# Attention and convolution under a written order on VectorE and ScalarE, with the sink as a column and the convolution's elementwise work off GpSimd

## The chip, the cores and the metric

The kernel runs on one core of a Trainium2 chip. The metric is the device time of one execution in microseconds. Three runs before the change gave 1163.16, 1163.87 and 1164.9 us, a median of 1163.87.

## The reference, cut to what matters

One layer of a diffusion backbone over 1024 latent tokens of width 1024, with 256 context tokens in front: a modulated RMSNorm; half of the width goes through attention in a window with a sink, the other half through a gated convolution of width 3; one output projection; then a mixture of 16 experts. The change lies in the attention, the convolution and the loads of the output projection's weights:

```python
scale = hd ** -0.5                                   # hd = 64: 0.125
s_loc = einsum('bnqkgd,bnjkd->bnkgqj', qb, kb) * scale        # |i - j| <= 128
s_ctx = einsum('bnqkgd,bjkd->bnkgqj', qb, k_ctx) * scale      # all 256 context keys
p = softmax(concatenate([sk, s_ctx, s_loc], axis=-1), axis=-1)   # sk: one sink value a head
out = einsum(..., p_ctx, v_ctx) + einsum(..., p_loc, vb)

u = cg * hv                                          # convolution
up = pad(u, ((0, 0), (1, 1), (0, 0)))
y = conv_w[0] * up[:, :-2] + conv_w[1] * up[:, 1:-1] + conv_w[2] * up[:, 2:]
return bg * y

x = x + gt1 * (concatenate([att, conv], axis=-1) @ w_out)
```

## The kernel before

All products are made of float32 operands split into a high and a low part of a faster type: the high part is a rounded copy (ScalarE), the low part the difference (VectorE or GpSimd), and three matmuls (high by high, high by low, low by high) stand for one. A tile's name with an h or an l at its end is its high or low part.

The stage of the change is the one in which attention and convolution are woven together. `attention()` (line 680) runs 33 rounds for 32 units; unit u is the query block b = u // 4 of 128 tokens and the head pair hp = u % 4. In round u the generators `scores(u)` and `values(u - 1)` are advanced alternately, six steps a round. `scores` multiplies the queries with 256 context keys and 256 or 384 latent keys into PSUM (`ps_s`, lines 563 and 565), once for each of the two heads; VectorE adds the mask and takes the row's maximum, sink included (line 575), ScalarE takes exp and its sum (line 578), a few instructions on two columns add the sink's share (lines 585 to 588), and the two heads are scaled, one on VectorE (line 594), one on ScalarE (line 592). `values` turns the probabilities on TensorE (`pt`, line 622) in two or three pieces, splits each piece (`pth`, high on ScalarE in line 625, low on VectorE in line 626), multiplies with the values (`po_att`, line 613) and joins the product's two halves: a copy on ScalarE (`up`, line 639) and two additions on VectorE (`attT`, line 643).

`conv()` (line 714) runs 12 parts: for each of four groups f of 128 channels the products for cg, hv and bg, each of two halves of 512 tokens with 8 steps of three matmuls (lines 730 to 732). `conv_load` (line 701) loads the next part's weights (`wcr`) and splits them whole: the high part on ScalarE, the low part on GpSimd (line 711). After hv the three taps are applied: line 755 and twice line 760 on GpSimd, line 759 on ScalarE. `weave` (line 815) advances attention and convolution in turn; after the last unit `prepare()` (line 798) takes attention's place: it loads the output weights in four pieces (`wo_load`: DMA, then a multiplication with the gate row in line 776, the tiles `wor`) and splits them (`wo_split`, lines 223 and 224, `woh` and `wol`). Then `project(0)` multiplies (line 879): the first 24 matmuls take pieces 0 and 1, the next 24 pieces 2 and 3.

In this stage the order on TensorE alone is that of the code (`manual_schedule(engines={ET.PE})`, line 94). On the other engines a scheduler sets it, by a timeline that it simulates while the kernel is built; at run time each engine takes its instructions in that order, and each waits for what it reads.

Of the kernel before, what the change touches and what calls it, by code (L numbers as in the profile page):

```python
# [85 lines left out]
def tile_layer(ctx, tc, x, c, cx, c_ctx, w_ada, b_ada, g_mix, w_in, conv_w, sink, w_out, g_ffn,  # L86
# [188 lines left out]
    nc.sync.dma_start(sinkb, sink.partition_broadcast(128).rearrange("p o h -> p (o h)"))  # L275
    nc.vector.tensor_scalar(sink8, sinkb, 8.0, None, op0=OP.mult)

# [262 lines left out]
    attT = {}  # L540
    negm = consts.tile([128, NT, NH], F32, name="negm")
    mx = consts.tile([128, NT, NH], F32, name="mx")
# [8 lines left out]
    def scores(u):  # L551
# [4 lines left out]
        loc = slice(blocks[0] * 128, (blocks[-1] + 1) * 128)  # L556
        sm2, s_sm = slots.get((2, 640), F32, "sm")
        for i in range(2):
# [37 lines left out]

    ptf = [0]

    def values(u):
        b, hp = divmod(u, 4)  # L600
        kv = hp // 2
# [33 lines left out]

        if b // 4 not in attT:
            attT[b // 4] = slots.get((4, 512), F32, "attT")
        up = work.tile([64, 2, 128], F32, tag="up", name="up")
        nc.scalar.copy(up.rearrange("p b c -> p (b c)"), po[64:128])
        pov = po.rearrange("p (b c) -> p b c", b=2)  # L640
        for par in range(2):
            dst = attT[b // 4][0][64 * par:64 * par + 64, hp, (b % 4) * 128:(b % 4 + 1) * 128]
            nc.vector.tensor_tensor(dst, pov[:64, par], up[:, par], op=OP.add)
        if b % 2 and hp == 3:
            slots.put(qT[b // 2][1])

# [33 lines left out]
    def attention():  # L680
        rc = router_consts()
        for u in range(4 * NT + 1):
            if u == 2:
                q_turn(NT - 1)
            if 20 <= u < 24:
                next(rc, None)
            sc = scores(u) if u < 4 * NT else iter(())
            va = values(u - 1) if u else iter(())

            for i, g in enumerate((sc, va, sc, va, va, va)):  # L690
                next(g, None)
                if i < 5:
                    yield 1
                if u == 0 and g is sc:
                    yield 1

# [4 lines left out]
    def conv_load(i):  # L701

        if i >= 12:
            return
        f, part = divmod(i, 3)
        raw = wm("wcr", (8, 128))
        c0 = conv_col[part] + f * 128
        nc.sync.dma_start(raw, win_v[:, :, c0:c0 + 128])
        wsp, s_w = slots.get((2, 8, 128), F32R, "wcs")
        nc.scalar.copy(wsp[:, 0], raw)  # L710
        nc.gpsimd.tensor_tensor(wsp[:, 1], raw, wsp[:, 0].bitcast(F32), op=OP.subtract)  # L711
        conv_w_of[i] = (wsp, s_w)

    def conv():
        st = {}
        conv_load(0)
        for i in range(12):
            f, part = divmod(i, 3)
            conv_load(i + 1)
            wsp, s_w = conv_w_of.pop(i)  # L720
            if part == 0:
# [4 lines left out]
            for half in range(2):  # L726
                ps = p1n("ps_cv")
                for k in range(KC):
# [3 lines left out]
                    mm(ps, wsp[:, 1, k], hi, start=False, stop=k == KC - 1)  # L732
                    yield 1
                tok = slice(half * 512, (half + 1) * 512)
# [5 lines left out]
                else:  # L740
                    if f == 2 and half == 0:
                        cvT[1] = slots.get((2, S), F32, "cvT")
                    dst = st["y"] if f == 0 else cvT[f // 2][0][:, f % 2]
                    nc.vector.tensor_tensor(dst[:, tok], ps, st["y"][:, tok], op=OP.mult)
            slots.put(s_w)
            if i == 2:
# [5 lines left out]
            if part == 1:  # L752
                y = st["cg"].rearrange("p a b -> p (a b)")
                u = st["u"]
# [14 lines left out]

    def wo_load(i):  # L770

        g, n = divmod(i, 2)
        cols = slice(n * 512, (n + 1) * 512)
        r, s_r = slots.get((4, 512), F32, "wor")
        nc.sync.dma_start(r, wout_v[:, 4 * g:4 * g + 4, cols])
        nc.vector.tensor_tensor(r, r, crow["gt1"][:, None, cols].to_broadcast([128, 4, 512]), op=OP.mult)
        wo[g, n] = [r, s_r]

# [19 lines left out]
    def prepare():  # L798
# [3 lines left out]
        bcast_row(crow["gt1"], rows_d[0])  # L802
        wo_load(0)
        yield 4
        wo_split(0)
        attended(0, ((0, 4),))
        wo_load(1)
        yield 8
        wo_split(1)
        attended(0, ((4, 2),))  # L810
        yield 6
        wo_load(2)
        yield 4

    weave([(steps(attention(), prepare()), 160.0), (conv(), 161.0)])

# [681 lines left out]
def _constants():  # L1498
# [10 lines left out]
    amask = np.zeros((128, 768), np.float32)  # L1509
    amask[:, 256:384] = np.where(j >= q, 0.0, NEG)  # L1510
    amask[:, 512:640] = np.where(j <= q, 0.0, NEG)
    amask = amask.astype(ml_dtypes.bfloat16)
# [33 lines left out]
```

## Time and profile before

| | |
|---|---|
| runs | 1163.16, 1163.87, 1164.9 us |
| the profiled execution | 1163.48 us, of which its instructions span 1161.7 us |
| TensorE busy in the span | 1058.4 us (91%) |
| VectorE, ScalarE, GpSimd busy | 967.2 (83%), 766.1 (66%), 351.0 us (30%) |
| attention and convolution | 178.4 to 433.7 us of the span |
| output projection, routing and sorting | 433.7 to some 560 us |
| experts | from there to the end |

A group's line gives its source line, engine, operation, what it writes and reads, its count, then its busy time, the mean duration of one, and the idle time of the engine just before it with what ended it. A timeline's line gives the start, the duration, the engine and the source line, and in brackets how long the engine had been idle and who released it. Matmuls overlap, so a matmul's duration is longer than its distance to the next.

### The profile page before, as it was taken

How to read it: one execution, taken by the hardware profiler on the slowest of the kernel's cores; microseconds unless marked ns; L12 is line 12 of the kernel's file. 1: busy time of each engine (PE TensorE's matmuls, PEld its weight loads, DVE VectorE, ACT ScalarE, POOL GpSimd, SP SyncE). 2: the span in 40 equal slices, each digit the busy share in tenths (PEclk: the TensorE clock that was granted, in tenths of full speed). 3: DMA queues.
4: the chain of work that ended last, by engine and by line, in shares of the span. 5: the costliest groups of instructions: out<-in, count | busy, mean ns of one | idle time of the engine just before them, and what ended most of it. 6: DMA issues, size and time to landing. Idle time of an engine off the chain costs nothing.

```text
span 1161.7 us, 15615 instructions
## 1 busy us (share of the span) xinstructions
PE 1058.4 (91%) x5486; PEld 873.5 (75%) x5486; DVE 967.2 (83%) x1661; ACT 766.1 (66%) x1058; POOL 351.0 (30%) x292
## 2 busy tenths in 40 slices
PE   6786889999899998999399999999999999999981
PEld 2675667888788877888288888888888888888861
DVE  7888455887878785389899999999999999999975
ACT  7565655767666643232288878878878877888853
POOL 0457681221303031222212433322333322330022
PEclk9897999999999999999599999999999999999996
DMA  9644440010101079648789999999999999999555
GB/s 376 232 164 144 164 146 19 24 33 1 55 1 37 19 278 339 181 127 270 273 322 356 399 403 390 391 388 389 395 404 392 389 389 389 394 404 390 203 195 221
DMA packets 90790, 292.89 MB, mean 252 GB/s; under 512 B 7044, under 2 KB 20816, under 8 KB 89688
## 3 DMA queue, kind: packets, MB, share of 16 engines
q1 hardware_dynamic: 84808, 270.40, 61.0%
q0 software_dynamic: 5904, 21.50, 7.7%
q8 instruction: 43, 0.70, 0.2%
q14 instruction: 35, 0.29, 0.1%
HBM read 266.69 MB, written 25.18 MB: 251 GB/s over the span
## 4 chain that ended last, share of the span: by engine, by line
PE 72%; DVE 13%; issue 5%; ACT 4%; DMA 4%; POOL 1%; POOLq 0%; ACTq 0%; DVEq 0%; SPq 0%
PE pg L1313 14%; PE pu L1313 14%; PE py L1313 13%; PE po L879 7%; PE ps_cv L731 3%; PE ps_cv L730 3%; PE ps_cv L732 3%; PE pt L622 2%; PE po_att L613 2%; DVE whl L1150 2%; PE ps_s L565 2%; PE xTp L1299 1%; PE ps_s L563 1%; PE pl L954 1%; PE hTtp L1299 1%
## 5 line engine op out<-in xcount | busy, mean ns | idle before, releaser
L1150 DVE TENSOR_TENSOR whl<-raw,whl 128x1024 fp32r<-128x1024 f32 x384 | 455.2, 1224 | 29.9 <-ACT whl L1147 18.9
L1147 ACT CAST whl<-raw 128x1024 fp32r<-128x1024 f32 x384 | 400.2, 1054 | 100.2 <-PE pu L1313 35.6
L1313 PE MATMUL pg<-whl,xT 128*128 128x512 f32 x768 | 186.2, 395 | 2.1 <-DVE whl L1150 2.1
L1313 PE MATMUL pu<-whl,xT 128*128 128x512 f32 x768 | 180.9, 392 | 0.0
L1313 PEld LDWEIGHTS pg<-whl,xT 128*128 128x128 f32 x768 | 142.3, 189 | 31.6 <-DVE whl L1150 2.9
L1313 PE MATMUL py<-whl,hTt 128*128 128x512 f32 x720 | 165.9, 389 | 0.0
L1313 PEld LDWEIGHTS pu<-whl,xT 128*128 128x128 f32 x768 | 143.0, 188 | 29.4
L1313 PEld LDWEIGHTS py<-whl,hTt 128*128 128x128 f32 x720 | 135.1, 188 | 28.4 <-DVE whl L1150 0.3
L1278 POOL TENSOR_SCALAR oh<-iota,pos 128x128 bf16<-128x128 f32 x104 | 100.5, 981 | 0.5
L1371 POOL DMA_INDIRECT acc_d<-yt,idx x15 | 38.5, 2565 | 196.0 <-DVE yt L1359 196.0
L1323 POOL DMA_INDIRECT xr<-h_d,idx x16 | 22.3, 1395 | 199.2 <-DVE gate_w L1289 199.2
L730 PE MATMUL ps_cv<-hTh,wcs 128*128 128x512 f32 x192 | 81.5, 424 | 0.0
L463 POOL TENSOR_TENSOR acc<-acc,wmod 128x1024 f32<-128x1024 f32 x28 | 70.0, 2518 | 27.8 <-ACT wmod L461 26.7
L625 ACT CAST pth<-pt 128x512 fp32r<-128x512 f32 (+1 forms) x88 | 46.1, 524 | 46.2 <-PE pt L622 46.1
L731 PE MATMUL ps_cv<-hTl,wcs 128*128 128x512 f32 x192 | 76.1, 397 | 0.0
L732 PE MATMUL ps_cv<-hTh,wcs 128*128 128x512 f32 x192 | 76.0, 396 | 0.0
L879 PE MATMUL po<-woh,ah 128*128 128x512 f32 x240 | 70.8, 404 | 0.6 <-ACT woh L223 0.6
L626 DVE TENSOR_TENSOR pth<-pt,pth 128x512 fp32r<-128x512 f32 (+1 forms) x88 | 53.9, 613 | 20.1 <-ACT pth L625 19.2
L711 POOL TENSOR_TENSOR wcs<-wcr,wcs 128x1024 fp32r<-128x1024 f32 x12 | 28.6, 2389 | 110.2 <-ACT wcs L710 87.5
L578 ACT ACTIVATE sm<-sm,negm 128x640 f32<-128x640 f32 (+1 forms) x64 | 51.6, 807 | 4.0 <-DVE negm L577 3.9
L575 DVE CUSTOM_DVE_ANT_0 sm<-ps_s,maskt,sink 128x640 f32<-128x640 f32 (+1 forms) x56 | 48.3, 863 | 6.9 <-PE ps_s L565 6.3
L879 PEld LDWEIGHTS po<-woh,ah 128*128 128x128 f32 x240 | 44.1, 191 | 9.4 <-ACT woh L223 1.0
(297 smaller groups left out, 1828.4 us busy)
## 6 DMA issues: line engine op xcount, KB each, us to landing
raw<-in_w_gate_dram SPq DMA_DIRECT2D x64, 1024.0 KB, 9.6
raw<-in_w_up_dram SPq DMA_DIRECT2D x64, 1024.0 KB, 7.8
raw<-in_w_down_dram SPq DMA_DIRECT2D x64, 1024.0 KB, 9.6
wmod<-in_w_ada_dram SPq DMA_DIRECT2D x32, 512.0 KB, 3.7
wa<-in_w_ada_dram SPq DMA_DIRECT2D x8, 1024.0 KB, 5.3
wcr<-in_w_in_dram SPq DMA_DIRECT2D x12, 512.0 KB, 3.8
xt<-in_x_dram SPq DMA_DIRECT2D x4, 1024.0 KB, 20.6
wor<-in_w_out_dram SPq DMA_DIRECT2D x4, 1024.0 KB
```

Source lines behind the costliest of these rows:

```text
L463: nc.gpsimd.tensor_tensor(acc, acc, wt, op=OP.add)
L575: nc.vector.tensor_tensor_reduce(dst, src, mk, op0=OP.add, op1=OP.max, scale=1.0, scalar=sink8[:, h:h + 1], accum_out=mx[:, b, h:h + 1])
L578: nc.scalar.activation(sm, sm, AF.Exp, bias=negm[:, b, h:h + 1], scale=0.125, accum_out=esum[:, b, h:h + 1])
L626: nc.vector.tensor_tensor(pth[:, 1, :n], pt[:, :n], pth[:, 0, :n].bitcast(F32), op=OP.subtract)
L730: mm(ps, wsp[:, 0, k], hi, start=k == 0, stop=False)
L731: mm(ps, wsp[:, 0, k], lo, start=False, stop=False)
L732: mm(ps, wsp[:, 1, k], hi, start=False, stop=k == KC - 1)
L879: mm(po[n], a, wo[k // 4, n][j][:, k % 4], start=first, stop=last)
L1147: nc.scalar.copy(w[:, 0], t[:, k % 2])
L1150: low = nc.vector.tensor_tensor(w[:, 1], t[:, k % 2], w[:, 0].bitcast(F32), op=OP.subtract)
L1278: nc.gpsimd.tensor_scalar(oh[:, t], iota1, pos[:, t, 0, e:e + 1], None, op0=OP.is_equal)
L1313: mm(ps[n], a_hl[:, a, k], w[:, j, n * 512:(n + 1) * 512], start=first, stop=last)
```

## The change

The sink becomes one more column of the scores, so the exp's own sum contains it and lines 585 to 587 go; the scale of -1/8 is multiplied into the queries, so the row's minimum serves directly as exp's bias and line 577 goes. The convolution's low parts and taps 1 and 2 move from GpSimd to VectorE, tap 0 to ScalarE, and the weights are split in halves at given steps of the part before. The order of VectorE and ScalarE in the woven stage is that of the code. In it the first head's exp stands with its scores, the second head's exp and the scaling stand one step later each, and the join of a unit's halves (`join`) is put into the next round, behind that round's first exp. `prepare()` issues the loads of the output weights apart from their gating.

```diff
@@ q_proj
-        nc.scalar.copy(qs[:, :, 0, :], tv)
-        nc.vector.tensor_tensor(qs[:, :, 1, :], tv, qs[:, :, 0, :].bitcast(F32), op=OP.subtract)
+        nc.scalar.activation(qs[:, :, 0, :], tv, AF.Copy, scale=-0.125)
+        nc.vector.scalar_tensor_tensor(qs[:, :, 1, :], tv, -0.125, qs[:, :, 0, :].bitcast(F32), op0=OP.mult,
+                                       op1=OP.subtract)
@@ scores
+        def exp(i):
+            h = 2 * hp + i
+            sx = sm2[:, i, :W + 1]
+            nc.scalar.activation(sx, sx, AF.Exp, bias=mx[:, b, h:h + 1], scale=-1.0,
+                                 accum_out=esum[:, b, h:h + 1])
...
-            nc.vector.tensor_tensor_reduce(dst, src, mk, op0=OP.add, op1=OP.max, scale=1.0,
+            if i == 0:
+                nc.vector.tensor_copy(sm2[:, :, W], sink8[:, hs])
+            nc.vector.tensor_tensor_reduce(dst, src, mk, op0=OP.add, op1=OP.min, scale=1.0,
                                            scalar=sink8[:, h:h + 1], accum_out=mx[:, b, h:h + 1])
-            nc.vector.tensor_scalar(negm[:, b, h:h + 1], mx[:, b, h:h + 1], -0.125, None, op0=OP.mult)
-            nc.scalar.activation(sm, sm, AF.Exp, bias=negm[:, b, h:h + 1], scale=0.125,
-                                 accum_out=esum[:, b, h:h + 1])
             if i == 0:
-                yield
-        hs = slice(2 * hp, 2 * hp + 2)
-        r = rec[:, b, hs]
-        nc.vector.tensor_tensor(r, sinkb[:, hs], negm[:, b, hs], op=OP.add)
-        nc.scalar.activation(r, r, AF.Exp)
-        nc.vector.tensor_tensor(r, r, esum[:, b, hs], op=OP.add)
-        nc.vector.reciprocal(r, r)
+                exp(0)
+            yield
+        exp(1)
+        yield
+        nc.vector.reciprocal(rec[:, b, hs], esum[:, b, hs])
@@ attention
-            for i, g in enumerate((sc, va, sc, va, va, va)):
-                next(g, None)
...
+            next(sc, None)
+            while joined:
+                joined.pop()()
+            yield 1
+            next(va, None)
+            yield 1
+            next(sc, None)
+            yield 1
+            next(va, None)
+            next(sc, None)
+            yield 1
...
+            next(va, None)
+            next(sc, None)
+            yield 1
+            next(va, None)
@@ conv_load, conv
+    def conv_split(i, low, n):
+        if i < 12:
+            raw, wsp, _ = conv_w_of[i]
+            ks = slice(4 * n, 4 * n + 4)
+            if low:
+                nc.vector.tensor_tensor(wsp[:, 1, ks], raw[:, ks], wsp[:, 0, ks].bitcast(F32), op=OP.subtract)
+            else:
+                nc.scalar.copy(wsp[:, 0, ks], raw[:, ks])
...
-        nc.scalar.copy(wsp[:, 0], raw)
-        nc.gpsimd.tensor_tensor(wsp[:, 1], raw, wsp[:, 0].bitcast(F32), op=OP.subtract)
...
+                    at = 8 * half + k
+                    if at in (7, 8, 9, 10):
+                        conv_split(i + 1, *divmod(at - 7, 2))
+                    if part == 2 and at in (1, 4):
+                        j = 1 if at == 1 else 2
+                        nc.vector.scalar_tensor_tensor(st["y"], st["u"][:, j:j + S], convT_w[:, 4 * j + f:4 * j + f + 1],
+                                                       st["y"], op0=OP.mult, op1=OP.add)
...
-                nc.gpsimd.tensor_scalar(y, u[:, 0:S], convT_w[:, f:f + 1], None, op0=OP.mult)
-                tap = wm("tap", (S,))
-                for j in (1, 2):
-                    w = convT_w[:, 4 * j + f:4 * j + f + 1]
-                    nc.scalar.activation(tap, u[:, j:j + S], AF.Copy, scale=w)
-                    nc.gpsimd.tensor_tensor(y, y, tap, op=OP.add)
+                nc.scalar.activation(y, st["u"][:, 0:S], AF.Copy, scale=convT_w[:, f:f + 1])
@@ prepare
-        wo_load(0)
+        wo_issue(0)
+        yield 5
+        wo_issue(1)
+        wo_gate(0)
+        attended(0, ((0, 4),))
         yield 4
         wo_split(0)
...
+        yield 5
+        wo_issue(2)
+        wo_gate(1)
+        attended(0, ((4, 2),))
+        yield 4
         wo_split(1)
...
-    weave([(steps(attention(), prepare()), 160.0), (conv(), 161.0)])
+    with tc.manual_schedule(engines={ET.PE, ET.DVE, ET.Activation}):
+        weave([(steps(attention(), prepare()), 160.0), (conv(), 161.0)])
```

Three places show how the order moves. First ScalarE in one round of the woven stage, before; `sm_2238` holds the scores of that round's unit, `pth` and `up` are of the unit before it.

```order
COPY up<-po_att 64x256
CAST pth<-pt 128x512
ACTIVATE sm_2238,esum<-sm_2238,negm 128x640
CAST pth<-pt 128x512
ACTIVATE sm_2238,esum<-sm_2238,negm 128x640
ACTIVATE rec<-rec 128x2
CAST pth<-pt 128x256
ACTIVATE sm_2238<-sm_2238,rec 128x640
```

The same of the changed kernel, in the round of unit 6 (`sm_1810`), into which one tap of the convolution falls (`cg<-u`).

```order
ACTIVATE sm_1810,esum<-sm_1810,mx 128x641
COPY up<-po_att 64x256
ACTIVATE cg<-u,smallT 128x1024
CAST pth<-pt 128x512 x2
ACTIVATE sm_1810,esum<-sm_1810,mx 128x641
CAST pth<-pt 128x256
ACTIVATE sm_1810<-sm_1810,rec 128x640
```

The copy `up` and the first `pth` stood ahead of the first exp; now the first exp stands ahead of both, and the tap between them.

Second, VectorE in a round before (`ISA` is the masked row maximum and the read of its accumulator; the round's last rows, a reciprocal and a scaling, are left out).

```order
ISA sm_2472,mx<-ps_s,maskt,sink_285 128x640
ISA mx 128x1
TENSOR_TENSOR attT_1531<-po_att,up 64x128 x2
TENSOR_SCALAR negm<-mx 128x1
TENSOR_TENSOR pth<-pt,pth 128x512
ISA sm_2472,mx<-ps_s,maskt,sink_285 128x640
ISA mx 128x1
TENSOR_SCALAR negm<-mx 128x1
TENSOR_TENSOR rec<-sinkb,negm 128x2
TENSOR_TENSOR pth<-pt,pth 128x512
TENSOR_TENSOR rec<-rec,esum 128x2
```

And VectorE in the changed kernel's round of unit 6.

```order
COPY sm_1810<-sink_285 128x2
ISA sm_1810,mx<-ps_s,maskt,sink_285 128x640
ISA mx 128x1
TENSOR_TENSOR attT_1546<-po_att,up 64x128 x2
TENSOR_TENSOR pth<-pt,pth 128x512
SCALAR_TENSOR_TENSOR cg<-u,smallT,cg 128x1024
ISA sm_1810,mx<-ps_s,maskt,sink_285 128x640
ISA mx 128x1
TENSOR_TENSOR pth<-pt,pth 128x512
TENSOR_TENSOR pth<-pt,pth 128x256
RECIPROCAL rec<-esum 128x2
TENSOR_SCALAR sm_1810<-sm_1810,rec 128x640
```

The small instructions on `negm` and `rec` are gone, a copy of two columns is new, and a tap of 1024 columns stands between the first `pth` and the second row minimum; the rest keeps its places.

Third, VectorE at the stage's end, before, from the last product `u` of the convolution on; `wor` are the output weights (3976 is piece 1, 3954 piece 0, 4037 and 4056 pieces 2 and 3).

```order
TENSOR_TENSOR u<-ps_cv,cg 128x512
TENSOR_TENSOR wol_3970<-wor_3954,woh_3969 128x2048
TENSOR_TENSOR wol_4012<-wor_3976,woh_4011 128x2048
TENSOR_TENSOR wor_4037<-wor_4037,rowsA_3952 128x2048
TENSOR_TENSOR wor_4056<-wor_4056,rowsA_3952 128x2048
TENSOR_TENSOR wol_4060<-wor_4037,woh_4059 128x2048
TENSOR_TENSOR cvT_3503<-ps_cv,cg 128x512 x2
TENSOR_TENSOR wol_4066<-wor_4056,woh_4065 128x2048
```

The same end in the changed kernel, after `u`, the row `rowsA<-rowsA,gf` and the low part of piece 0; 3942 is piece 3, 3856 piece 1, 3898 piece 2, and `cg` the taps.

```order
SCALAR_TENSOR_TENSOR cg<-u,smallT,cg 128x1024
TENSOR_TENSOR wor_3942<-wor_3942,rowsA_3833 128x2048
SCALAR_TENSOR_TENSOR cg<-u,smallT,cg 128x1024
TENSOR_TENSOR wor_3856<-wor_3856,rowsA_3833 128x2048
TENSOR_TENSOR ah_3859<-cvT_2062,ah_3859 128x256
TENSOR_TENSOR cvT_3401<-ps_cv,cg 128x512
TENSOR_TENSOR wol_3918<-wor_3856,woh_3917 128x2048
TENSOR_TENSOR wor_3898<-wor_3898,rowsA_3833 128x2048
TENSOR_TENSOR cvT_3401<-ps_cv,cg 128x512
TENSOR_TENSOR ah_3859<-cvT_3401,ah_3859 128x256
TENSOR_TENSOR wol_3952<-wor_3942,woh_3951 128x2048
TENSOR_TENSOR wol_3946<-wor_3898,woh_3945 128x2048
```

Before, both low parts of pieces 0 and 1 and their gating were done at this point; now the gating of piece 3 and two taps stand ahead of the gating of piece 1, and the low part of piece 2 is the last.

## Rows read from the trace of the kernel before


**Rows 1.** The page's first part: busy time of each engine, its share of the span and its instructions, over the whole execution.

```profile
PE 1058.4 (91%) x5486; PEld 873.5 (75%) x5486; DVE 967.2 (83%) x1661; ACT 766.1 (66%) x1058; POOL 351.0 (30%) x292
```

**Rows 2.** Busy time by stretch: the woven stage up to the first matmul of the output projection, and the 16 us after it. Columns: stretch and its length, busy time of PE, PEld, DVE, ACT, POOL with instructions, granted TensorE clock, DMA share, GB/s.

```profile
178.40:433.70 255.30, 247.94 (x1466) 213.29 (x1467) 197.98 (x510) 164.93 (x345) 56.76 (x23) 0.99 0.15 50
433.70:450.00 16.30, 12.82 (x48) 9.87 (x47) 13.97 (x14) 6.60 (x9) 0.01 (x1) 0.90 1.02 404
```

**Rows 3.** The waits of TensorE from 178 to 434 us: who waited for whom, us in total, times, the longest.

```profile
PE po_att L613 <- DVE pth L626: 5.1, 8, 1.1
PE ps_s L563 <- DVE bias L489: 2.2, 1, 2.2
PE pt L622 <- DVE sm L594: 1.9, 2, 1.5
PE po_att L613 <- ACT pth L625: 0.2, 1, 0.2
```

**Rows 4.** The timeline of all engines from 291 us: start, duration, engine, line, what is written and read, in brackets the idle time before and its releaser.

```profile
291.63 2.37 POOL L760 TENSOR_TENSOR cg<-cg,tap 128x1024 f32<-128x1024 f32 x1
291.70 2.33 DVE L587 TENSOR_TENSOR rec<-rec,esum 128x2 f32<-128x2 f32 x1
...
294.96 0.30 PE L622 MATMUL pt<-ident,sm 128*128 128x128 f32 x1 [1.45 <-DVE sm L594]
```

**Rows 5.** VectorE's timeline at the end of the woven stage.

```profile
423.00 0.69 DVE L738 TENSOR_TENSOR u<-ps_cv,cg 128x512 f32<-128x512 f32 x1
423.91 7.55 DVE L224 TENSOR_TENSOR wol<-wor,woh 128x2048 fp32r<-128x2048 f32 x2 [0.21 <-ACT woh L223]
431.38 6.68 DVE L776 TENSOR_TENSOR wor<-wor,rowsA 128x2048 f32<-128x2048 f32 x2
437.98 2.28 DVE L224 TENSOR_TENSOR wol<-wor,woh 128x2048 fp32r<-128x2048 f32 x1
...
441.38 2.27 DVE L224 TENSOR_TENSOR wol<-wor,woh 128x2048 fp32r<-128x2048 f32 x1
```

**Rows 6.** TensorE's timeline there.

```profile
443.71 0.50 PE L879 MATMUL po<-wol,ah 128*128 128x512 f32 x1 [2.87 <-DVE wol L224]
...
445.96 1.91 PE L879 MATMUL po<-woh,ah 128*128 128x512 f32 x4
```

**Rows 7.** TensorE's timeline in a round into which nothing of the convolution falls on the other engines.

```profile
249.87 0.40 PE L563 MATMUL ps_s<-kcv,qT 128*128 128x256 f32 x2
250.10 0.52 PE L565 MATMUL ps_s<-kx,qT 128*128 128x384 f32 x2
...
256.10 0.88 PE L613 MATMUL po_att<-pth,vx 128*128 128x256 f32 x6
...
256.81 0.40 PE L563 MATMUL ps_s<-kcv,qT 128*128 128x256 f32 x2
```

**Rows 8.** VectorE's timeline in the same round.

```profile
250.51 0.58 DVE L643 TENSOR_TENSOR attT<-po_att,up 64x128 f32<-64x128 f32 x2 [0.56 <-ACT up L639]
251.12 0.88 DVE L575 CUSTOM_DVE_ANT_0 sm<-ps_s,maskt,sink 128x640 f32<-128x640 f32 x1
...
252.41 0.69 DVE L626 TENSOR_TENSOR pth<-pt,pth 128x512 fp32r<-128x512 f32 x1 [0.20 <-ACT pth L625]
...
256.12 0.41 DVE L626 TENSOR_TENSOR pth<-pt,pth 128x256 fp32r<-128x256 f32 x1
```

**Rows 9.** ScalarE's timeline in the same round.

```profile
250.11 0.37 ACT L639 COPY up<-po_att 64x256 f32<-64x256 f32 x1
...
252.27 0.83 ACT L578 ACTIVATE sm<-sm,negm 128x640 f32<-128x640 f32 x1
...
255.70 0.37 ACT L625 CAST pth<-pt 128x256 fp32r<-128x256 f32 x1
```

**Rows 10.** Groups by form on VectorE, ScalarE and GpSimd from 178 to 448 us: line, engine, operation, form and count, then busy time, mean ns of one, and idle time before with what ended it.

```profile
L711 POOL TENSOR_TENSOR wcs<-wcr,wcs 128x1024 fp32r<-128x1024 f32 x10 | 23.9, 2392 | 107.9 <-ACT wcs L710 85.2 <-PE po_att L613 22.7
...
L587 DVE TENSOR_TENSOR rec<-rec,esum 128x2 f32<-128x2 f32 x32 | 12.0, 376 | 5.2 <-ACT rec L586 4.5
...
L577 DVE TENSOR_SCALAR negm<-mx 128x1 f32<-128x1 f32 x64 | 9.8, 152 | 2.0
L759 ACT ACTIVATE tap<-u,smallT 128x1024 f32<-128x1024 f32 x8 | 9.2, 1150 | 5.2 <-POOL cg L760 4.4 <-DVE u L738 0.6 <-DVE rec L587 0.2
L585 DVE TENSOR_TENSOR rec<-sinkb,negm 128x2 f32<-128x2 f32 x32 | 9.0, 282 | 1.0
...
L738 DVE TENSOR_TENSOR u<-ps_cv,cg 128x512 f32<-128x512 f32 x8 | 5.5, 684 | 0.2
...
L736 ACT COPY cg<-ps_cv 128x512 f32<-128x512 f32 x8 | 4.6, 579 | 3.2 <-PE ps_cv L732 3.2
...
L796 DVE TENSOR_TENSOR ah<-attT,ah 128x512 fp32r<-128x512 f32 x3 | 2.0, 679 | 0.0
L795 ACT CAST ah<-attT 128x512 fp32r<-128x512 f32 x3 | 1.9, 620 | 2.1 <-DVE wol L224 2.1
...
L834 DVE SCALAR_TENSOR_TENSOR rowsA<-rowsA,gf 128x1024 f32<-128x1024 f32 x1 | 1.2, 1210 | 0.0
```

**Rows 11.** ScalarE's timeline at the end of the woven stage.

```profile
435.94 1.92 ACT L223 CAST woh<-wor 128x2048 fp32r<-128x2048 f32 x1 [5.45 <-DVE wor L776]
```

**Rows 12.** From the chain that ended last, 423 to 446 us: start, duration, what.

```profile
425.71 5.48 DMA wor<-in_w_out_dram
```

More of the change, by code (lines that the diff above doesn't have):

```diff
@@ L275, in tile_layer @@
     nc.sync.dma_start(sinkb, sink.partition_broadcast(128).rearrange("p o h -> p (o h)"))
[L276 removed]
+    nc.vector.tensor_scalar(sink8, sinkb, -1.0, None, op0=OP.mult)
     def hT_slots(n, name):
@@ L556, in scores @@
         loc = slice(blocks[0] * 128, (blocks[-1] + 1) * 128)
-        sm2, s_sm = slots.get((2, 640), F32, "sm")
+        hs = slice(2 * hp, 2 * hp + 2)
+        sm2, s_sm = slots.get((2, 648), F32, "sm")
+        def exp(i):
[3 more added lines that the diff above has]
+                                 accum_out=esum[:, b, h:h + 1])
         for i in range(2):
@@ L597, in tile_layer @@
     ptf = [0]
+    joined = []
     def values(u):
@@ L634, in values, with join @@
             flush()
[L636 to L645, printed above, removed]
+        def join():
+            if b // 4 not in attT:
+                attT[b // 4] = slots.get((4, 512), F32, "attT")
+            up = work.tile([64, 2, 128], F32, tag="up", name="up")
+            nc.scalar.copy(up.rearrange("p b c -> p (b c)"), po[64:128])
+            pov = po.rearrange("p (b c) -> p b c", b=2)
+            for par in range(2):
+                dst = attT[b // 4][0][64 * par:64 * par + 64, hp, (b % 4) * 128:(b % 4 + 1) * 128]
+                nc.vector.tensor_tensor(dst, pov[:64, par], up[:, par], op=OP.add)
+            if b % 2 and hp == 3:
+                slots.put(qT[b // 2][1])
+        joined.append(join)
     rt = {}
@@ L688, in attention @@
             va = values(u - 1) if u else iter(())
-            for i, g in enumerate((sc, va, sc, va, va, va)):
-                next(g, None)
[L692 to L695, printed above, removed]
+            next(sc, None)
[9 more added lines that the diff above has]
+            yield 1
+            if u == 0:
+                yield 1
+            next(va, None)
+            next(sc, None)
+            yield 1
+            next(va, None)
+        joined.pop()()
     cvT = {}
@@ L701, in conv_load @@
     def conv_load(i):
[L703 to L709, printed above, removed]
-        nc.scalar.copy(wsp[:, 0], raw)
-        nc.gpsimd.tensor_tensor(wsp[:, 1], raw, wsp[:, 0].bitcast(F32), op=OP.subtract)
-        conv_w_of[i] = (wsp, s_w)
+        if i < 12:
+            f, part = divmod(i, 3)
+            raw = wm("wcr", (8, 128))
+            c0 = conv_col[part] + f * 128
+            nc.sync.dma_start(raw, win_v[:, :, c0:c0 + 128])
+            conv_w_of[i] = [raw, *slots.get((2, 8, 128), F32R, "wcs")]
+    def conv_split(i, low, n):
+        if i < 12:
+            raw, wsp, _ = conv_w_of[i]
[4 more added lines that the diff above has]
+                nc.scalar.copy(wsp[:, 0, ks], raw[:, ks])
+    conv_load(0)
+    for q in range(4):
+        conv_split(0, *divmod(q, 2))
     def conv():
         st = {}
-        conv_load(0)
         for i in range(12):
@@ L719, in conv @@
             conv_load(i + 1)
-            wsp, s_w = conv_w_of.pop(i)
+            _, wsp, s_w = conv_w_of.pop(i)
             if part == 0:
@@ L732, in conv @@
                     mm(ps, wsp[:, 1, k], hi, start=False, stop=k == KC - 1)
-                    yield 1
+                    at = 8 * half + k
[5 more added lines that the diff above has]
+                                                       st["y"], op0=OP.mult, op1=OP.add)
+                    if k < KC - 1:
+                        yield 1
                 tok = slice(half * 512, (half + 1) * 512)
@@ L744, in conv @@
                     nc.vector.tensor_tensor(dst[:, tok], ps, st["y"][:, tok], op=OP.mult)
+                yield 1
             slots.put(s_w)
@@ L768, in tile_layer, with wo_issue, wo_gate @@
     ah_of = {}
-    def wo_load(i):
[L772 to L777, printed above, removed]
+    def wo_issue(i):
+        g, n = divmod(i, 2)
+        wo[g, n] = slots.get((4, 512), F32, "wor")
+        nc.sync.dma_start(wo[g, n][0], wout_v[:, 4 * g:4 * g + 4, n * 512:(n + 1) * 512])
+    def wo_gate(i):
+        r = wo[divmod(i, 2)][0]
+        cols = slice(i % 2 * 512, i % 2 * 512 + 512)
+        nc.vector.tensor_tensor(r, r, crow["gt1"][:, None, cols].to_broadcast([128, 4, 512]), op=OP.mult)
+    def wo_load(i):
+        wo_issue(i)
+        wo_gate(i)
     def wo_split(i):
@@ L1509, in _constants @@
     amask = np.zeros((128, 768), np.float32)
-    amask[:, 256:384] = np.where(j >= q, 0.0, NEG)
-    amask[:, 512:640] = np.where(j <= q, 0.0, NEG)
+    amask[:, 256:384] = np.where(j >= q, 0.0, -NEG)
+    amask[:, 512:640] = np.where(j <= q, 0.0, -NEG)
     amask = amask.astype(ml_dtypes.bfloat16)
```

9 lines of the change are left out of this document (1 added, 8 removed).

## The prediction

> **What bounds the kernel now.** I read the busy times first: TensorE works 1058.4 of the span's 1161.7 us, no other engine more than 967 [rows 1]. The stretches come next: in the woven stage TensorE works 247.9 of 255.3 us at a granted clock of 0.99, and in the 16.3 us after it 12.8, at 0.90 [rows 2]. So the stage is TensorE's, with VectorE (198.0) and ScalarE (164.9) having room on average; what the change can win in the stage is at most the waits, and what it can lose is any chain through the other engines that grows longer than TensorE's work of a round. TensorE's waits show which: 5.1 us of `po_att` on the low part `pth`, 1.9 of `pt` on the scaling, 0.2 on a cast [rows 3], 7.2 in all; the 2.2 on `bias` lie before the weave and stay. The timeline names the cause: an addition on two columns took 2.33 us on VectorE while GpSimd's tap addition of 2.37 us ran beside it, and TensorE then idled 1.45 us behind the scaling [rows 4]. Line 587 takes 376 ns on average and line 585 282 ns, line 577, as small but with one tensor as input, 152 [rows 10]. At the stage's end VectorE's two low parts took 7.55 us and two gatings 6.68, where single ones take 2.27 [rows 5]: (7.55 + 6.68) − 4 × 2.28 = 5.1 us lost beside GpSimd's taps; TensorE then waits 2.87 us for the last `wol` [rows 6].
>
> TensorE's matmuls are as many as before, in nearly the same order. Behind the stage the experts keep it at work, so I pass a shift of the stage's end on to the kernel's end in full.
>
> **What goes.** GpSimd leaves the weave, and with it the waits of 7.2 us, if nothing takes their place. VectorE also loses two instructions of 152 ns, one of 282 and one of 376 a unit (1.0 us with their stretching), ScalarE one small exp; but VectorE gains 24 half low parts of 0.68 us (as line 796, the same form) for ten of GpSimd's 2.39 and eight taps of 1.21 (as line 834), while ScalarE gives up eight taps of 1.15 for four, and splits in halves of 0.62 [rows 10]. These sums stay below TensorE's time; the order decides.
>
> **What comes: a loop through three engines.** An engine takes its instructions in order. In the new order one thing follows another within a round, with no way round it: the row minimum of head 0 on VectorE, exp of head 0 and then `up` on ScalarE, the two `attT`, the first low `pth` and the row minimum of head 1 on VectorE, exp of head 1 and then the third cast `pth` on ScalarE, the third low `pth` on VectorE, the last `po_att` on TensorE, and only then the next unit's scores, which that row minimum waits for. Before, `up` and the first cast stood ahead of the exp, so `up` came 0.24 us into the round and `attT` stood ahead of the row maximum without holding anything [rows 7 to 9].
>
> Its length from these rows, from the first score matmul at 249.87: the scores are complete after 0.75 (250.10 + 0.52); then 0.88 (minimum), 0.83 (exp), 0.37 (`up`), 0.58 (`attT`), 0.69 (low part), 0.88, 0.83, 0.37, 0.41: 6.6 us, and 0.03 to 0.06 for each hand-over between engines (250.48 to 250.51, 256.07 to 256.12), less the overlaps of neighbours on one engine: I take 6.83 [rows 7 to 9]. TensorE's round lasts 256.81 − 249.87 = 6.94, and it wants the third low part for the last of the six `po_att` matmuls, 0.12 apart, at 256.10 + 5 × 0.12 = 256.7, that is after 6.83. So the loop and TensorE's round are equal: without anything added no wait, but no slack either. In the old order the extras of the convolution were absorbed; now each that stands on the loop moves the round's end by its duration.
>
> I therefore count, from the written order, what stands on it in units 4 to 27, where the convolution falls (start to start 0.60 for a low half, `u` or a product `cvT`; 1.13 for a tap on VectorE, 0.52 for a half on ScalarE, 1.05 for the tap there, all a little under the durations of [rows 10]):
> VectorE between `attT` and the second row minimum, at the full price: seven low halves 4.3, two `u` 1.2, two `cvT` 1.2, two taps 2.3, and the tap on ScalarE in unit 6 0.93, together 9.9. VectorE behind the scaling, where some 0.2 is free: four halves 1.6, two `u` 0.8, two taps 1.9, together 4.3. ScalarE ahead of the third cast: four halves 2.1, one copy `cg` 0.47, one tap 1.05, together 3.6. Between the second and third low part, where about 0.57 is free: two taps 1.0, two halves 0.6. A half on ScalarE before the first `pth` 0.4, and about 0.95 for fractions of the others. Sum 20.8 us. The bounds: nothing, if each finds a gap (below), and 7.5 more if TensorE's clock also falls.
>
> **The stage's end.** On the clock of before, `u` ends at 423.7 [rows 5]. ScalarE's tap and its first `woh` (1.92) end at 426.7 [rows 11], the low part of piece 0 (2.27) at 428.9, a tap at 430.0. Then the gating of piece 3 stands in line, and I take its transfer to land as the last one does now, at 431.2 [rows 12]; gating 433.4, tap 434.6, gating of piece 1 436.8, its `woh` 438.7, its low part 441.0, gating of piece 2 443.2, two `cvT` and two low parts (1.3 and 4.5) 449.0. The last `wol` is now ready at 443.7 (441.38 + 2.27) [rows 5]: +5.3 us. The bounds: −2.8 if GpSimd's 5.1 goes and two taps of 1.13 come with no transfer in the way; +5.3 as worked out.
>
> **The sum.** The profiled execution took 1163.48 us, its span 1161.7, the median of the runs is 1163.87. 1163.48 − 7.2 + 20.8 + 5.3 = 1182.4; forecast 1182.
>
> **The rivals.**
> *The loop with room.* If a round has 0.5 us that I don't see (a hand-over shorter, a matmul's record late), each unit pays only what exceeds 0.5: by units that is 10.8, so 1163.48 − 7.2 + 10.8 + 5.3 = 1172.4. For it: many extras are single ones of 0.5 to 0.6. Against it: the loop's durations are the rows' own.
> *Faster: GpSimd was the only cause.* If the loop is shorter by a whole extra, the 7.2 go, nothing comes, and the end gains 2.8: 1153.5. For it: the waits lie beside GpSimd's work [rows 4], and both engines have time on average [rows 2]. Against it: an in-order chain doesn't use averages. It decides from a slack of about 1.1 us a round on. The Trainium skill, "SBUF — State Buffer", section "Who interferes with whom", speaks for this rival: it says that a two-input VectorE instruction and GpSimd working on SBUF exclude one another. Rows 4 agree (2.33 us against 152 ns for the small one).
> *Slower still: the clock falls.* After the idle 2.87 us four matmuls took 1.91 us where they take about 0.9 at full rate, in a stretch granted 0.90 [rows 2, 6]; that is about 1.4 us by the seven that ran so. If the added waits bring that four times in the weave, 5.6, and late weights of the convolution 2, the time is 1190. Against it: most of the new waits are below 1 us, like those of before, beside which the clock stood at 0.99.
> That the change misses its purpose, with GpSimd still in the weave, the order rules out: its low parts and taps are gone from there.
>
> **Numbers.** The forecast 0.54, the loop with room 0.21, the clock 0.11, faster 0.14. About 0.2% (2.3 us) is what a measurement here can tell from none. Faster holds the 0.14; of the loop with room 0.05 lies within 0.2% (a slack of about 0.9 a round); slower the other 0.81. The range is 1163 to 1194: it leaves out the faster rival and some 0.06 above, and covers the extras from a half to their full price and the clock. The forecast's own range is 1176 to 1188.
>
> **What would show it.** If right: VectorE idle before `attT`, released by `up`, 1.2 us a round, some 38 us in the stage; TensorE's waits of `po_att` on the low `pth` near 20 us, in rounds with a half, `u` or a tap; no two-column instruction of 2 us any more; the first matmul of the projection 13 to 14 us later, and then some 5 us more of waits on `woh` and `wol`. If the rival with room: waits only in rounds with a tap. If the faster one: under 2 us of waits in the weave. Wrong altogether would be an experts' stage that takes up or adds to the shift, or waits on scores rather than `pth`.

## The result and the profile after

The changed kernel took 1180.78 us, median of four runs (1179.93 to 1183.32), against 1163.8 of the kernel before (1163.16 to 1164.9): the ratio is 1.0149, interval 1.0131 to 1.0166. It is slower by 1.5%; 1182 was forecast. The profiled execution took 1180.33 us, its span 1178.5.

The page's busy times of the changed kernel, as in [rows 1]:

```profile
PE 1066.6 (90%) x5486; PEld 872.4 (74%) x5486; DVE 953.5 (81%) x1597; ACT 764.3 (65%) x1034; POOL 290.6 (25%) x268
```

VectorE, ScalarE and GpSimd are all less busy than before, the last by 60 us, and the kernel is slower. TensorE is busier by 8 us for the same 5486 instructions. By stretch (columns as in [rows 2]), up to the projection's first matmul and the 16 us behind it:

```profile
177.90:445.60 267.70, 256.45 (x1466) 213.91 (x1466) 183.93 (x444) 163.26 (x322) 1.85 (x10) 1.00 0.15 50
445.60:462.00 16.40, 8.54 (x27) 5.98 (x25) 15.37 (x11) 7.25 (x7) 0.00 (x0) 0.69 1.03 410
```

The woven stage grew from 255.3 to 267.7 us, GpSimd works 1.9 in it instead of 56.8. The clock stayed whole in it; after the stage it is 0.69 where it was 0.90. TensorE's waits in the changed kernel from 178 to 455 us, beside [rows 3]:

```profile
PE po L928 <- ACT woh L223: 6.8, 1, 6.8
PE po_att L621 <- DVE pth L634: 5.3, 12, 0.9
PE po_att L621 <- ACT pth L633: 1.6, 3, 0.6
PE pt L630 <- DVE pth L634: 1.6, 4, 0.6
PE ps_s L572 <- DVE bias L489: 1.3, 1, 1.3
```

In the weave that is 8.5 us of waits, hardly more than the 7.2 of before, while the stage is 12 us longer. The rest shows in two other places. One is the waits of the weight loads (PEld, 178 to 446 us):

```profile
PEld po_att L621 <- DVE pth L634: 11.8, 27, 1.1
PEld pt L630 <- DVE pth L634: 7.0, 12, 1.1
PEld po_att L621 <- ACT pth L633: 3.8, 9, 0.8
```

For `po_att` that is 15.6 us. The loads of the kernel before waited 8.0, 0.9 of it on casts:

```profile
PEld po_att L613 <- DVE pth L626: 7.1, 10, 1.3
```

The other is the matmuls' own records, which stretch: six `po_att` took 0.88 us in [rows 7]; in the changed kernel's round from 246 us, in which a product `cvT` falls, 1.44, of which about 0.5 is waiting for the low part inside what counts as busy (the fifth and the sixth, which waited, have records of 0.38 us each instead of 0.28, and the record of the one before runs on over the first 0.16 us of a wait):

```profile
251.96 1.44 PE L621 MATMUL po_att<-pth,vx 128*128 128x256 f32 x6
253.24 0.40 PE L572 MATMUL ps_s<-kcv,qT 128*128 128x256 f32 x2
```

So the 256.45 − 247.94 = 8.5 us that TensorE is "busy" for longer are no work: the matmuls are the same 1466. (The Trainium skill, "Perfetto Trace Analysis", says in its opening note that matmul busy time is a bad measure of how close a kernel is to its roofline, because matmuls are pipelined. The trace agrees that it misleads: here it holds these 8.5 us.) The chain that ended last, in that round, is the forecast loop, piece by piece (start, duration, what; "issue" is time with no wait in the profile):

```profile
246.29 0.88 DVE sm L587
247.21 0.93 ACT sm L564 x2
248.16 0.38 ACT up L649
248.56 0.28 DVE attT L653
248.86 0.28 DVE attT L653
249.17 0.69 DVE cg L786
249.87 0.59 DVE pth L634
...
252.25 0.27 ACT pth L633
252.53 0.44 DVE pth L634
253.01 0.39 PE po_att L621
253.40 0.24 PE ps_s L572 x2
```

Minimum, exp, `up`, `attT`, here a product of the convolution (`cg`), the first low part, and at the end the third cast, the third low part, the last `po_att` and the next scores. The row minimum and exp of head 1 lie in the stretch left out.

To measure stages, the tables below count the weave from the first to the last of the 576 convolution matmuls (`ps_cv`), and the tail from there to the start of the 48th matmul of the projection, where all four pieces of the weights have been used. What lies ahead of the weave differs between the profiled executions by up to 5.5 us (it starts at 177.0 to 182.5) and is left out that way.

| profiled execution | weave | tail |
|---|---|---|
| before | 254.0 | 16.6 |
| changed | 265.6 | 22.1 |

The end came 16.9 us later: 11.6 in the weave, 5.6 in the tail, 0.3 later at the weave's start, and 0.6 given back behind. The experts' stage passed the shift on unchanged, as was assumed: its first matmul is 17.54 us later, its last 17.47.

### The profile page after: what moved, and what is told of

The parts are those of the page before. It is cut to its first block, busy times and chain, and to the rows that moved or that the text cites. A ratio compares the mean times of both kernels' runs of the same rounds, so it can differ in the third digit from the quotient of the medians.

```text
span 1178.5 us, 15458 instructions
## 1 busy us (share of the span) xinstructions
PE 1066.6 (90%) x5486; PEld 872.4 (74%) x5486; DVE 953.5 (81%) x1597; ACT 764.3 (65%) x1034; POOL 290.6 (25%) x268
## 4 chain that ended last, share of the span: by engine, by line
PE 64%; DVE 18%; ACT 7%; DMA 6%; issue 4%; POOL 1%; POOLq 0%; ACTq 0%; DVEq 0%; SPq 0%
PE pg L1362 14%; PE pu L1362 14%; PE py L1362 13%; PE po L928 7%; DVE sm L587 3%; ACT sm L564 2%; DVE pth L634 2%; DMA xt<-in_x_dram 2%; DVE whl L1199 2%; PE po_att L621 2%; PE xTp L1348 1%; PE ps_cv L763 1%; PE ps_cv L764 1%; PE ps_cv L765 1%; PE pl L1003 1%
## 5 line engine op out<-in xcount | busy, mean ns | idle before, releaser
L564 ACT ACTIVATE sm<-sm,mx 128x641 f32<-128x641 f32 (+1 forms) x64 | 51.7, 808 | 54.5 <-DVE mx L587 53.2
L633 ACT CAST pth<-pt 128x512 fp32r<-128x512 f32 (+1 forms) x88 | 46.0, 524 | 15.6 <-PE pt L630 14.6
L928 PEld LDWEIGHTS po<-woh,ah 128*128 128x128 f32 x240 | 44.5, 193 | 15.6 <-ACT woh L223 7.2
```

What stands on the lines that cost most here:

```text
L564: nc.scalar.activation(sx, sx, AF.Exp, bias=mx[:, b, h:h + 1], scale=-1.0, accum_out=esum[:, b, h:h + 1])
L928: mm(po[n], a, wo[k // 4, n][j][:, k % 4], start=first, stop=last)
```

## The experiments

The theory is that of the prediction: the written order makes a loop through three engines as long as TensorE's round, and what the convolution puts on it is paid in full. The first rival is load: VectorE and ScalarE got GpSimd's work, which would cost the same in any order. The second is that GpSimd's work beside VectorE is what costs. Each kernel was timed against the kernel before on the same chip; the table at the end has all times.

**exp put back.** One step order of `scores` and one more advance in `attention`:

```diff
+            yield
             if i == 0:
                 exp(0)
-            yield
+                yield
@@ attention
             next(va, None)
+            next(sc, None)
             yield 1
             next(sc, None)
```

> The changed kernel, but exp of the first head stands behind the join and behind the first cast of the round (as it stood before the change); all work and TensorE's order are the same. Serial-loop theory: the loop from one row minimum to the next is shorter by about 1.3 us a round, most of the convolution's extras fall into that room, the first matmul of the output projection comes 8 to 14 us earlier than in the changed kernel (at 445.6 there), total 1167 to 1173 us. Rival, that VectorE and ScalarE simply carry too much (low parts and taps): the same work is done, so no change, 1179 to 1182 us.

Measured 1160.85 us, ratio to before 0.9958 (0.9936 to 0.998): some 20 us faster than the changed kernel, 6 more than was expected, and faster than the kernel before. The weave is 244.6 us, 21.0 less than changed and 9.4 less than before. Its waits of TensorE, 177 to 423 us:

```profile
PE ps_s L572 <- DVE bias L489: 1.3, 1, 1.3
PE po_att L622 <- ACT pth L634: 0.4, 2, 0.2
```

Nothing on the low parts is left. The stretch up to the projection's first matmul, with the columns of [rows 2]:

```profile
177.40:423.75 246.35, 244.56 (x1465) 212.59 (x1466) 184.26 (x444) 158.01 (x322) 1.52 (x7) 1.00 0.16 54
```

TensorE is busy for 11.9 us less than in the changed kernel's stretch, and for nearly all of the stage. All instructions are the same; in the two traces TensorE's order is the same too, and VectorE's but for a few fills of a column. Load is not the cause, one instruction's place on ScalarE is.

**The scheduler's order, with all the rest of the change.**

```diff
-    with tc.manual_schedule(engines={ET.PE, ET.DVE, ET.Activation}):
+    with tc.manual_schedule(engines={ET.PE}):
         weave(
```

> The changed kernel without its written order in the woven stage: VectorE and ScalarE stand in the scheduler's order again, TensorE's order and all work stay. Serial-loop theory: the loss of the weave goes (about 12 us), and with GpSimd out of the way the weave may even end before 433.7; total 1160 to 1170 us, by how the tail falls. Rival, load: the extra instructions on VectorE and ScalarE cost the same in any order, 1178 us or more.

Measured 1168.27 us, 1.0015 (0.9994 to 1.0035). The weave is 255.2 us, about as before the change (254.0), not shorter. Its waits, 178 to 436 us:

```profile
PE po_att L621 <- DVE pth L634: 5.1, 9, 1.4
PE ps_s L572 <- DVE bias L489: 1.3, 1, 1.3
PE pt L630 <- DVE pth L634: 1.3, 1, 1.3
PE po_att L621 <- ACT pth L633: 0.4, 1, 0.4
```

The loss of the weave goes with the written order, as the theory has it, but its second half ("may even end before") fails: `po_att` waits 5.1 us, to the tenth what it did in [rows 3] with GpSimd at work. The change without its written order, GpSimd's work taken out included, was worth nothing: waits of the scheduler's new order took the place of the old ones. What taking GpSimd out alone is worth was not tried.

**The low parts on GpSimd**, in the changed order:

```diff
-                nc.vector.tensor_tensor(wsp[:, 1, ks], raw[:, ks], ...
+                nc.gpsimd.tensor_tensor(wsp[:, 1, ks], raw[:, ks], ...
```

> The changed kernel, but the 24 half low parts of the convolution's weights are done on GpSimd (in the halves of the change); the taps stay on VectorE and ScalarE, the written order too. Serial-loop theory: some 6.5 us of the extras counted on the loop go, so 1172 to 1177 us. Rival, that GpSimd beside VectorE costs as much as it frees: 1180 us or more, with two-input instructions on VectorE stretched beside it.

Measured 1174.69 us, 1.0072 (1.0048 to 1.0095); the weave 258.3, that is 7.3 us less than changed. Of the 24 half low parts 22 fall into the weave; each had cost 7.3 / 22 = 0.3 us on average, about half its duration. The rival falls: what GpSimd stretched beside it (at the end) did not cost what was freed.

**Which buffers the weights' pieces get.** In the changed kernel piece 0, which is gated first, got the buffer of the last unit's scores, and its load was issued as the third of four:

```diff
-        slots.put(s_kc, s_vx, *s_kx)
+        slots.put(*s_kx, s_kc, s_vx)
...
+        slots.free_list.append(slots.free_list.pop(0))
         wo_issue(0)
```

> The changed kernel, but the output weights' pieces 0 and 1 get the buffers that come free first, so that both are issued ahead of piece 2; piece 0 waited for the last unit's scores buffer. Theory of the tail as a chain of loads, gatings and splits on VectorE: the gating of piece 0 starts near 431 instead of 435, TensorE's wait for woh falls from 6.8 to about 3 us, and the end comes 3 to 4 us earlier, 1176 to 1178 us; the weave stays. Rival: the last low part is bound by VectorE's own work and the later loads, so the first wait gets shorter and a later one longer, 1180 us as before.

Measured 1178.98 us, 1.0105 (1.0068 to 1.0142), just above what was expected; the intervals of this and of the changed kernel overlap. The profile decides: the tail is 19.1 instead of 22.1 us, TensorE's wait for `woh` 2.7 instead of 6.8, with 2.6 on `wol` in its place; the weave is the same 265.7. This execution began its weave 2.8 us later than that of the changed kernel, hence no gain in its span.

**Both together.** The two edits above.

> The exp put back behind the join and the first cast (as in the run e1_exp_back) together with the buffers of pieces 0 and 1 chosen so that both loads are issued first (as in e4_tail). If weave and tail are two separate terms, they add up: the weave ends as in e1_exp_back, 10 us before that of the kernel before, and the first row block of the projection 3 us earlier than there; 1157 to 1159 us. Rival, that the tail is bound by VectorE's own work behind those loads: 1160 to 1161, as e1_exp_back alone.

Measured 1158.24 us, 0.9936 (0.9916 to 0.9956): weave 244.7, tail 19.1. The two terms add up.

**And the tail's order written out**, on top of those two edits, with the code behind the weave taken into the same block:

```diff
+        wo_issue(1)
         yield 5
-        wo_issue(1)
         wo_gate(0)
         attended(0, ((0, 4),))
-        yield 4
+        wo_gate(1)
         wo_split(0)
+        yield 4
         yield 5
         wo_issue(2)
-        wo_gate(1)
         attended(0, ((4, 2),))
-        yield 4
         wo_split(1)
         yield 4
         wo_gate(2)
+        yield 4
```

> As e5_both, and the tail's order written out in the same block: the gatings of pieces 0 and 1 and the split of piece 0 stand ahead of the last u, the gating of piece 3 behind that of piece 2, the product of the routing row (S2) behind all splits; the same work. By the durations of the rows the last low part is then ready near 434 on the clock of e1_exp_back (440.4 there), the first row block ends some 6 us earlier than in e1_exp_back: 1153 to 1157 us. Rival, that loads or TensorE's lower clock after its idle time bound the tail: 1158 us or more.

Measured 1155.82 us, 0.9917 (0.9885 to 0.9949), the fastest of all, faster than both kernels. The tail is 17.7 us. Its waits of TensorE, 420 to 445 us:

```profile
PE po L931 <- ACT woh L223: 2.2, 1, 2.2
PE po L931 <- DVE wol L224: 1.8, 1, 1.8
```

and the two ends of the chain of gatings and splits on VectorE:

```profile
411.37 2.29 DVE L819 TENSOR_TENSOR wor<-wor,rowsA 128x2048 f32<-128x2048 f32 x1
...
433.68 2.29 DVE L224 TENSOR_TENSOR wol<-wor,woh 128x2048 fp32r<-128x2048 f32 x1
```

The last low part is ready at 436.0, which is 434.5 on the clock of the run with the exp put back (its weave ended 1.5 us earlier), where near 434 was expected. Of the expected 6 us 4.6 came (22.3 to 17.7); TensorE's clock in the 15.7 us from 425.3 on was 0.78.

**Only the join put first**, the exp still ahead of the first cast:

```diff
+            next(sc, None)
             yield 1
             next(va, None)
```

with exp of head 0 as a step of its own, as in the first experiment.

> The changed kernel, with only the join put ahead of the first exp again; the exp still stands ahead of the first cast. The loop is then shorter by about 0.45 us a round instead of 1.3. Serial-loop theory with room per round: of the extras what exceeds 0.45 us a unit stays, about half, so the weave ends 8 to 12 us earlier than in the changed kernel, total 1169 to 1173 us, between the changed kernel and e1_exp_back. Rival, that one of the two moves alone does it (the join waits for exp, and nothing else matters): 1160 to 1162, as e1_exp_back; or, if only the cast matters, 1179 to 1182.

Measured 1167.86 us, 1.0013 (0.9999 to 1.0027), 1 us below what was expected. The weave is 252.1: 13.5 us less than changed, 7.5 more than with the exp put back. Both moves count; the first makes room of about half a microsecond a round. The rounds of units 8, 9 and 24 fall to TensorE's 6.95 us with it, those of units 5, 14 and 17, with more on the loop, only by 0.50, 0.57 and 0.48.

**exp put back, low parts on GpSimd.**

> The kernel of e1_exp_back with the 24 half low parts on GpSimd as in e3_low_gpsimd. Serial-loop theory: the extras lie in room that the round has now, so taking them from VectorE gives nothing in the weave: its end within 1 us of e1_exp_back, total 1159 to 1162 us (in the changed order the same move gave about 6 us). Load theory: VectorE's work is on the path in any order, so some 3 to 6 us earlier again, 1155 to 1158.

Measured 1160.45 us, 0.9959 (0.9946 to 0.9972), weave 244.6: no change from 244.6. The same move that gave 7.3 us in the changed order gives nothing here.

**A needless instruction on the loop**, in the changed order and with the exp put back:

```diff
                 nc.vector.tensor_tensor(dst, pov[:64, par], up[:, par], op=OP.add)
+            for _ in range(2):
+                nc.vector.tensor_tensor(up, up, up, op=OP.subtract)
```

> The changed kernel with two needless subtractions of 64x256 on VectorE behind each join (they overwrite the copy up with zeros after its last reader), some 0.7 us a round, on the loop. Serial-loop theory: the changed order has no room, so each round grows by nearly all of it: 31 rounds by 0.5 to 0.7 us, the woven stage 14 to 20 us longer than in the changed kernel, 1195 to 1201 us. Rival, that the loop has room of half a microsecond or more in most rounds: below 8 us more.

> The kernel of e1_exp_back with the same two needless subtractions. Serial-loop theory: the room of about 1.3 us a round falls to about 0.6, so rounds without an extra of the convolution keep TensorE's 6.95 us and only rounds with one pay: 3 to 7 us longer than e1_exp_back, 1164 to 1168 us. Rival, that VectorE's work is paid in any order: 14 us or more, 1175 us.

In the changed order it took 1206.46 us, 1.0333 (1.0298 to 1.0368); the weave grew by 19.1 us to 284.7, within what was expected, and of the 24 rounds of units 4 to 27 21 grew by 0.77 to 0.80. The total is above what was expected: 5.7 us more came in the experts' stage, where `py` waited once 3.3 us for a weight; that was not followed up. With the exp put back it took 1166.16 us, 0.9993 (0.9969 to 1.0017), the weave 250.2, 5.6 more than without. The clearest reading is the round of unit 19, into which no extra of the convolution falls, from its first score matmul to the next unit's. In the changed kernel 331.29 − 324.17 = 7.12 us:

```profile
324.17 0.41 PE L572 MATMUL ps_s<-kcv,qT 128*128 128x256 f32 x2
...
331.29 0.40 PE L572 MATMUL ps_s<-kcv,qT 128*128 128x256 f32 x2
```

the same round with the needless instructions, 342.98 − 335.08 = 7.90 us:

```profile
335.08 0.40 PE L572 MATMUL ps_s<-kcv,qT 128*128 128x256 f32 x2
...
342.98 0.40 PE L572 MATMUL ps_s<-kcv,qT 128*128 128x256 f32 x2
```

and with the exp put back and the needless instructions, 318.52 − 311.57 = 6.95, TensorE's own time as in [rows 7]:

```profile
311.57 0.40 PE L572 MATMUL ps_s<-kcv,qT 128*128 128x256 f32 x2
...
318.52 0.40 PE L572 MATMUL ps_s<-kcv,qT 128*128 128x256 f32 x2
```

The two subtractions (0.42 us each) cost 0.78 in the one order and nothing in the other. In this round the changed order has no room at all; the other has at least 0.78 us.

| kernel | time, us | ratio to before | weave | tail |
|---|---|---|---|---|
| exp put back | 1160.85 | 0.9958 | 244.6 | 22.3 |
| scheduler's order | 1168.27 | 1.0015 | 255.2 | 19.1 |
| low parts on GpSimd | 1174.69 | 1.0072 | 258.3 | 21.2 |
| buffers of the pieces | 1178.98 | 1.0105 | 265.7 | 19.1 |
| exp back and buffers | 1158.24 | 0.9936 | 244.7 | 19.1 |
| and the tail written out | 1155.82 | 0.9917 | 244.7 | 17.7 |
| join first only | 1167.86 | 1.0013 | 252.1 | 23.4 |
| exp back, low parts on GpSimd | 1160.45 | 0.9959 | 244.6 | 23.5 |
| changed, needless work | 1206.46 | 1.0333 | 284.7 | 22.6 |
| exp back, needless work | 1166.16 | 0.9993 | 250.2 | 22.1 |

## Why the prediction was right, step by step

**The loop.** Right as a mechanism, and shown: it is the chain that ended last in the round from 246 us, VectorE's idle time ahead of `attT` behind `up` is 42.1 us in 32 rounds (some 38 were forecast), and the exp's place alone moves the weave by 21 us. The round was 0.18 us short: without extras it takes 7.12 us, not 6.94. ScalarE's and VectorE's timelines of the changed kernel show where:

```profile
325.88 0.83 ACT L564 ACTIVATE sm<-sm,mx 128x641 f32<-128x641 f32 x1 [1.00 <-DVE mx L587]
326.62 0.19 ACT L564 ACTIVATION_READ_ACCUMULATOR sm<-sm,mx 128x1 f32 x1
326.83 0.37 ACT L649 COPY up<-po_att 64x256 f32<-64x256 f32 x1
```

```profile
324.96 0.88 DVE L587 CUSTOM_DVE_ANT_0 sm<-ps_s,maskt,sink 128x640 f32<-128x640 f32 x1 [0.31 <-PE ps_s L574]
...
330.58 0.42 DVE L634 TENSOR_TENSOR pth<-pt,pth 128x256 fp32r<-128x256 f32 x1 [0.65 <-ACT pth L633]
```

The scores are ready 0.79 us into the round and the third low part ends at 331.00, 6.83 after 324.17, which is the forecast figure to the hundredth (exp is longer by its accumulator's read, the overlaps on VectorE give that back). What was wrong is the last step: from there to the next unit's scores, at 331.29, it takes 0.29 us, where 0.12 was taken from `po_att` matmuls that run on without a wait. The last `po_att` starts 0.06 after the low part's end, and the next matmul 0.22 to 0.23 behind it instead of 0.12:

```profile
331.06 0.39 PE L621 MATMUL po_att<-pth,vx 128*128 128x256 f32 x1
```

That is the whole difference.

**The extras.** 20.8 us was forecast for them; the whole loss against the kernel with the exp put back is 265.6 − 244.6 = 21.0. The agreement is partly luck. The loop itself is over TensorE's round by 0.18, over 24 units about 4 us that had not been counted; and with the exp put back some extras are still paid, about 4 us above 6.95. Added up round by round for units 4 to 27 (without unit 21, which takes 8.75 us even with the exp put back), what lies above 7.12 us is 18.6: that is what the extras there cost. About 2 us more were lost in units 1, 28 and 30, which had not been counted. The forecast charged every one its full price; the low parts, priced at 6.5 for those that GpSimd would take, gave 7.3.

**What goes.** The term that was mis-sized most: 7.2 us of waits were taken as all that could be won, and with the exp put back the weave is 9.4 shorter than before. TensorE's idle time in it falls from 7.3 to 0.9 us, which is 6.4; the other 3.0 come out of its busy time. About 1.2 of these are the clock: in the profiled execution of before, the first six convolution matmuls start 0.43 us apart, in the changed kernel and with the exp put back 0.23 apart; TensorE had waited 2.2 us on `bias` just ahead of them, in the others 1.3. The first 4 us of the weave, before (partly at the lower level of the clock, 1.2 GHz) and changed (all at 2.4 GHz):

```profile
179.43:183.43 4.00, 4.00 (x14) 3.16 (x14) 0.91 (x3) 2.10 (x3) 0.00 (x0) 0.68 0.31 92
179.72:183.72 4.00, 4.00 (x22) 3.37 (x21) 2.01 (x7) 1.92 (x4) 0.00 (x0) 1.00 0.03 6
```

At the same clock the changed weave would so be about 12.8 us longer than that of before, not 11.6. The remaining 1.8 are most likely waits hidden in stretched matmuls, as above: the matmuls are the same in number and form.

Who causes the waits was also only half right. In the kernel before, the six of line 585 that ran beside an instruction of GpSimd took 0.81 us on average (0.16 the others), the six of line 587 1.32 (0.16), but the minimum, the low parts `pth` and `attT`, which read PSUM, were not longer at all, before or in the experiment with GpSimd's half low parts (0.69 and 0.69 for `pth`). The rounds of units 16, 18 and 26, in each of which line 587 stood beside GpSimd, are together 5.7 us longer than with the exp put back, which speaks for GpSimd as a cause there. Yet with these instructions and GpSimd gone, the scheduler's order still had its 5.1 us of waits. So what was won belongs to the order of the first experiment together with the removal of GpSimd's work and of the small instructions; how much to each was not tried.

**The tail.** +5.3 forecast, +5.6 measured, but from other parts than were named: the agreement is luck. The gating of piece 3 stood ahead of that of piece 1, as forecast, but found its data there; VectorE waited 3.34 us for piece 0 instead and 1.42 for the row `gf`:

```profile
435.11 2.29 DVE L817 TENSOR_TENSOR wor<-wor,rowsA 128x2048 f32<-128x2048 f32 x1 [3.34 <-DMA wor<-in_w_out_dram]
440.03 1.23 DVE L883 SCALAR_TENSOR_TENSOR rowsA<-rowsA,gf 128x1024 f32<-128x1024 f32 x1 [1.42 <-DMA gf<-in_g_ffn_dram]
...
458.04 4.49 DVE L224 TENSOR_TENSOR wol<-wor,woh 128x2048 fp32r<-128x2048 f32 x2
```

The step that failed is "I take its transfer to land as the last one does now": the order of the loads had changed too, and was not looked at. The written tail shows that some 4.4 of the 5.6 us were order and buffers (22.1 to 17.7).

**The rivals.** The loop with room of 0.5 us falls: 7.12 and 7.90 us a round. The faster rival needed 1.1 us of room and had none; with the exp put back there is room, and the kernel is faster. The clock did not fall in the weave (1.00); in the tail it did, to 0.69, behind the idle 6.8 us.

**Of what would show it**, two signs failed. TensorE's waits of `po_att` on the low part are 5.3 us, not near 20; the rest of the loss stands in the waits of the weight loads and in stretched matmuls. And the projection's first matmul came 11.9 us later (433.68 to 445.57), not 13 to 14, because more was won than the 7.2 us. The others held: no instruction on two columns takes more than 0.17 us, and the projection waits 8.2 us on `woh` and `wol` where it waited 3.5.

## What to carry to other kernels

When an order is written out by hand over several engines, follow one item of work round the engines until it comes back to where it began, add up the durations on the way, and compare that sum with the bounding engine's time for a round: the difference is the room, and what is added on the way beyond it is paid, however idle the engines are on average. Here moving work to another engine gave 7.3 us in the weave without room and nothing with it; moving one instruction gave 21. And read the loads' order and buffers together with the order of what uses them.

## What was not expected

A matmul group's record holds waiting: the same six `po_att` show 0.88 us or 1.44, the same 1466 matmuls 247.9 us of busy time or 256.5. A wait's table alone would have said that the weave had lost 1.3 us (8.5 against 7.2) where it had lost 11.6.

GpSimd beside VectorE stretched, of the attention's instructions, the additions of two columns with both inputs in SBUF and, less, the scaling of one SBUF tensor of 640 columns by a column, 0.55 us without and 0.80 on average with GpSimd's half low parts beside it (at most 0.88); none that read PSUM. In the kernel before, of the twelve additions that ran beside GpSimd, eleven ended within 0.03 us of the end of the GpSimd instruction: they lasted until it was done, up to 2.33 us where one alone takes 0.16.
